# Opening weight tiles by contraction block, the last four heads projected together, rotary products on VectorE

## The chip, the cores and the metric

The kernel runs on one core of a Trainium2 chip. The metric is the device time of one execution in microseconds (us). Engines are named as in the profile: PE (TensorE, matmuls), PEld (its weight loads), DVE (VectorE), ACT (ScalarE), POOL (GpSimd) and SP (SyncE, which issues most of the DMAs).

## The reference, cut to what matters

One sequence of 512 tokens of width 1024 passes two layers. Both have a half-step SwiGLU at each end and a gated input embedding; the mixer between is a gated linear recurrence (HGRN2) in the first layer and latent attention with 16 heads in the second.

```python
for li in range(2):
    x = x + 0.5 * swiglu(rmsnorm(x, g[0]), ffn_w_in[li, 0], ffn_w_out[li, 0])
    h = rmsnorm(x, g[1])
    x = x + (hgrn2(h) if li == 0 else mla(h))
    x = x + 0.5 * swiglu(rmsnorm(x, g[2]), ffn_w_in[li, 1], ffn_w_out[li, 1])
    x = x + sigmoid(rmsnorm(x, g[3]) @ ple_w_gate[li]) * (p[li] @ ple_w_in[li])
return rmsnorm(x, final_norm)

def mla(h):                                   # k_nope, k_rope, v: made after layer 0
    c_q = rmsnorm(h @ w_dq, q_norm)           # 1024 -> 512
    q = (c_q @ w_uq).reshape(16, 128 + 64)    # per head: plain part, rotary part
    qr = concat(q1 * cos - q2 * sin, q2 * cos + q1 * sin)
    s = (q_nope @ k_nope.T + qr @ k_rope.T) * 192 ** -0.5
    return softmax(causal(s)) @ v  ->  @ w_out   # 16 heads of 128 -> 1024
```

All is float32.

## The kernel before

**Numbers.** Each float32 operand is split into a rounded part `hi` and a rest `lo`; a product is three matmuls, hi·hi, lo·hi and hi·lo (`mm3`, lines 151 to 153). `x` lies transposed, as eight tiles `x[m]` of 128 features by 512 tokens. `split` makes `hi` on ACT and `lo` on DVE (lines 166 and 167; with a gain 169 and 170).

**Weights.** The host packs all weights into 512 KB tiles of eight 128x128 blocks, in the order in which they are used (`_stream`). A tile comes by DMA into one of 5 `raw` buffers, ACT casts it to `whi`, DVE subtracts to get `wlo` (3 buffers each; lines 129 and 130, in the feed-forward parts 304 and 305). `chain` gives one 128x512 output block: for each of its input blocks an `mm3` into one of four "mm" PSUM banks. Four more banks are the "aux" ones.

**Norms.** `Stats` adds up squares of tiles (ACT squares, L183, and adds on DVE or POOL, L188). `column_sums` transposes the sum on PE (L214) and reduces it on DVE (L216); `columns` turns that into a factor (DVE L195, POOL L198); `rows` spreads it on PE (L222) and copies it out on ACT (L229). In a chain the factor is applied to the output, so that PE need not wait for it.

**Opening.** The first four output blocks of the first feed-forward part (`primed`) are made in a block of its own, whose SP and PE orders are as written (`manual_schedule`). A weight tile holds the eight input blocks of one output block, so that a tile of 512 KB is whole only for one bank. Squares are summed on PE, by 64 one-column matmuls against `ones` (`square`, L1222).

**Latent attention** (`mla`) isn't written in a fixed order: a list scheduler places its instructions by what is ready and by the order of the program. Four heads share a rotary group (`rope`): two chains, copies to SBUF (L1084, L1085), four products with cos and sin (L1086, L1090 on DVE, L1087, L1091 on POOL), a difference and a sum (L1088, L1092), splits. For head h, `scores` (h) runs ahead of `weigh` (h-1): scores in four tiles with softmax (L1142 mask and maximum on DVE, L1149 exponential on ACT, L1151 on DVE, L1152 on POOL), then transposes of the probabilities (L1163) and the product with the values. `project` multiplies a pair of heads with its part of `w_out` and adds it to `x` (L1185); for the last pair each tile is at once prepared for the next feed-forward part (`post`: split L169/L170, squares L183/L188). Between the scores of head 15 and its transposes lie the whole projection of heads 12 and 13, 48 matmuls, and part of what came before.

Of the kernel before, what the change touches and what calls it, by code (L numbers as in the profile page):

```python
# [9 lines left out]
F32 = mybir.dt.float32  # L10
F32R = mybir.dt.float32r
I32 = mybir.dt.int32
AF = mybir.ActivationFunctionType
# [3 lines left out]
P = 128  # L17
T = 512
NT = T // P
D = 1024  # L20
# [37 lines left out]
def kernel(  # L58
# [27 lines left out]
    def slot(s="s", dt=F32, tag="s"):  # L86
        return spool.tile([P, T], dt, tag=tag, bufs=BUFS[tag], name=name(s))
# [147 lines left out]
    def load(c):  # L235
        nc.sync.dma_start(x[c], xT[c * P : (c + 1) * P, :])
# [342 lines left out]
        stream["n"] = (stream["tiles"] - 2) * WB  # L579

    class Next:
        def __init__(self, cols, eng=pool):
            self.cols = cols
            self.xg = [[] for _ in cols]
            self.stats = Stats(KC, eng)

        def __call__(self, m):
            for i, col in enumerate(self.cols):
                self.xg[i].append(split(x[m], gain(col, m)))
            if self.stats.eng is not None:  # L590
                self.stats.add(x[m])

    def gcol(layer, i):
        return V_GAIN + (layer * 4 + i) * KC
# [471 lines left out]

    def mla(xg, stats, cn, krope, sin, cos, post):
        _, rb = rows(stats)
        st = Stats(4)
        cq = []  # L1070
        for m in range(4):
            ps = chain(xg)
# [3 lines left out]
            cq.append(split(c, gain(V_QN, m)))  # L1076
        rq = st.columns()
        sc = tiny()
        dve.tensor_scalar(out=sc, in0=rq, scalar1=float(192.0 ** -0.5), scalar2=None, op0=ALU.mult)

        def rope(group):
            pa, pb = chain(cq), chain(cq)
            qa, qb, ta, tb = (slot("rt") for _ in range(4))
            act.copy(qa, pa)  # L1084
            act.copy(qb, pb)  # L1085
            dve.tensor_tensor(out=ta, in0=qa, in1=cos, op=ALU.mult)  # L1086
            pool.tensor_tensor(out=tb, in0=qb, in1=sin, op=ALU.mult)  # L1087
            dve.tensor_tensor(out=ta, in0=ta, in1=tb, op=ALU.subtract)  # L1088
            h1, l1 = split(ta)
            dve.tensor_tensor(out=qb, in0=qb, in1=cos, op=ALU.mult)  # L1090
            pool.tensor_tensor(out=qa, in0=qa, in1=sin, op=ALU.mult)  # L1091
            dve.tensor_tensor(out=qb, in0=qb, in1=qa, op=ALU.add)  # L1092
            h2, l2 = split(qb)
            res = []
            for j in range(4):
                d = slot("qr", F32R)
                s = slice(32 * j, 32 * j + 32)
                for i, src in enumerate((h1, h2, l1, l2)):
                    nc.sync.dma_start(d[32 * i : 32 * i + 32, :].bitcast(F32), src[s, :].bitcast(F32))
                res.append(d)  # L1100
            return res
# [76 lines left out]

        outs = []

        def project(n, part):
            pair = outs[2 * n : 2 * n + 2]
            for m in range(part * KC // 2, (part + 1) * KC // 2):
                po = chain(pair[::-1] if n < B_HEADS // 2 - 1 else pair)
                dve.tensor_tensor(out=x[m], in0=po, in1=x[m], op=ALU.add)  # L1185
                if n == B_HEADS // 2 - 1:
                    post(m)

        qr, vals = rope(0), values(0)
        last = None  # L1190
        for h in range(B_HEADS):
            ahead = h < B_HEADS - 1
            rotated, value = qr[h % 4], vals[h % 2]
            if h % 4 == 3 and ahead:
                qr = rope(h // 4 + 1)
            if h % 2 == 1 and ahead:
                vals = values(h // 2 + 1)
            pr = scores(rotated)
            if last is not None:
                outs.append(weigh(*last))  # L1200
            last = (pr, value)
            if h > 2:
                project((h - 1) // 2 - 1, 1 - h % 2)
        project(B_HEADS // 2 - 2, 1)
        outs.append(weigh(*last))
        for part in range(2):
            project(B_HEADS // 2 - 1, part)


    first = Next([gcol(0, 0)], None)  # L1210
    primed, heads = [mm_bank() for _ in range(4)], []

    def prime(c, *ks):
        for k in ks:
            w = tuple(a[:, k * P : (k + 1) * P] for a in heads[c])
            mm3(primed[c], w, first.xg[0][k], k == 0, k == KC - 1)

    def square(m):
        sq = slot("sq", F32, "r")
        act.activation(sq, x[m], AF.Square)  # L1220
        for j in range(NT):
            pe.matmul(  # L1222
                dots[:, j : j + 1], sq[:, j * P : (j + 1) * P], ones, start=m + j == 0, stop=m == KC - 1,
                skip_group_check=True,
            )

    def head(pieces=1):
        fetch(pieces)
        heads.append(stream["ready"].pop(0))
        stream["n"] += WB  # L1230

    with tc.manual_schedule(engines={mybir.EngineType.SP, mybir.EngineType.PE}):
        dots = aux_bank()
        nc.sync.dma_start(vc, vec)
        load(0)
        first(0)
        head(4)
        prime(0, 0)
        square(0)
        for m in range(1, KC):  # L1240
            load(m)
            first(m)
            if m == 1:
                square(1)
            if m == 2:
                head(2)
                prime(0, 1, 2)
                prime(1, 0, 1, 2)
            if m == 4:
                head(2)  # L1250
                for c in range(2):
                    prime(c, 3, 4)
                prime(2, *range(5))
            if m in (2, 4):
                for k in (m - 1, m) if m == 4 else (m,):
                    square(k)
            if m == 5:
                nc.sync.dma_start(cs, cst)
            if m > 4:
                for c in range(3):  # L1260
                    if m < KC - 1:
                        prime(c, m)
                square(m)
        sums = dots[:, 0:NT]
        for c in range(3):
            prime(c, KC - 1)
        head()
# [48 lines left out]
def _rows(w):  # L1316
    k, m = w.shape
    return w.reshape(k // P, P, m // P, P).transpose(0, 2, 1, 3).reshape(-1, P, P)


def _stream(i):
    out = []

    def ffn(l, n):
        wi = i["ffn_w_in"][l, n]
        wo = i["ffn_w_out"][l, n]
        sides = [_blocks(wi[:, c : c + DFF]).reshape(NF, KC, P, P) for c in (0, DFF)]
        for lo, hi in GROUPS:
            for f in range(lo, hi):
                if f < PLAIN:  # L1330
# [55 lines left out]
    def project(n, part):  # L1386
        a, b, c = 2 * n * P, (2 * n + 1) * P, (2 * n + 2) * P
        rows = [wo[a:b], wo[b:c]]
        if n < B_HEADS // 2 - 1:
            rows = rows[::-1]  # L1390
        out.append(_blocks(np.concatenate(rows, axis=0)[:, part * D // 2 : (part + 1) * D // 2]))

    for h in range(B_HEADS):
        ahead = h < B_HEADS - 1
        if h % 4 == 3 and ahead:
            turned(h // 4 + 1)
        if h % 2 == 1 and ahead:
# [3 lines left out]
        if h > 2:  # L1401
            project((h - 1) // 2 - 1, 1 - h % 2)
    project(B_HEADS // 2 - 2, 1)
    for part in range(2):
        project(B_HEADS // 2 - 1, part)
    ffn(1, 1)
    ple(1)
    w = np.concatenate(out, axis=0)
# [64 lines left out]
```

## Time and profile before

| what | value |
|---|---|
| three runs | 2190.23, 2191.95, 2192.36 us; median 2191.95 |
| the profiled execution | 2192.49 us; its span 2190.7, so 1.8 lies around the span |
| busy share of the span | PE 99%, PEld 88%, DVE 69%, ACT 44%, POOL 15% |
| chain that ended last | PE 95%, DVE 3%, issue 1%, ACT 1% |
| DMA | 261.47 MB, 119 GB/s over the span |

The chain is followed back from the last instruction to what released each step; where a share of it belongs to PE, nothing but fewer or quicker matmuls shortens the span, and where it belongs to another engine PE stood waiting. Matmul ends are modelled, so a start-to-start distance of two equal matmuls tells more of their price than the length of one. PE's granted clock is in the views by window.

### The profile page before, as it was taken

To read this page: it belongs to the slowest core of one execution; us is meant where nothing else is said; L and a number is where in the kernel's file an instruction comes from. 1 tells how busy PE (TensorE), PEld (TensorE's weight loads), DVE (VectorE), ACT (ScalarE), POOL (GpSimd) and SP (SyncE) were. 2 spreads that over 40 slices of the span, in tenths; PEclk is the share of its full clock that TensorE was granted. 3 is DMA by queue.
4 is the path that set the end of the run, shared out by engine and by line. 5 is a ranking of instruction groups with operands and counts; after the bars stand their busy time and mean duration, and the time that the engine had idled before them with its cause. 6 is when DMAs were issued, how large, how long until landed. Compare 5 with 4: busy or idle time off the path is not lost.

```text
span 2190.7 us, 32865 instructions
## 1 busy us (share of the span) xinstructions
PE 2162.3 (99%) x13086; PEld 1935.8 (88%) x13086; DVE 1522.2 (69%) x2252; ACT 968.2 (44%) x1373; POOL 330.7 (15%) x437
## 2 busy tenths in 40 slices
PE   8999999999999999999999999999999999999998
PEld 7899998898888899998888989988888878999987
DVE  5777676777786676675766757767677776675765
ACT  5344353323235353454553525445454553443443
POOL 2000001554521000001110000022111110000011
PEclk9999999999999999999999999999999999999999
DMA  5465562212113565552234656422122134664621
GB/s 184 136 154 158 133 172 99 86 60 68 68 68 97 148 162 155 147 159 97 94 118 130 164 149 165 134 98 86 66 79 87 59 88 125 156 171 126 173 106 49
DMA packets 76106, 261.47 MB, mean 119 GB/s; under 512 B 9136, under 2 KB 11312, under 8 KB 75952
## 3 DMA queue, kind: packets, MB, share of 16 engines
q1 hardware_dynamic: 64720, 220.15, 30.5%
q0 software_dynamic: 10368, 37.75, 10.0%
q8 instruction: 103, 1.69, 0.3%
q10 hardware_dynamic: 864, 1.46, 0.2%
q14 instruction: 51, 0.42, 0.1%
HBM read 253.04 MB, written 2.10 MB: 116 GB/s over the span
## 4 chain that ended last, share of the span: by engine, by line
PE 95%; DVE 3%; issue 1%; ACT 1%; DMA 0%; POOL 0%; SPq 0%; DVEq 0%; ACTq 0%
PE aux L314 19%; PE mm L151 18%; PE mm L152 18%; PE mm L153 17%; PE mm L314 14%; PE aux L152 2%; PE aux L153 2%; PE aux L151 2%; PE aux L723 1%; PE aux L1163 1%; PE aux L1137 0%; PE aux L1138 0%; PE aux L214 0%; PE aux L1222 0%; PE aux L222 0%
## 5 line engine op out<-in xcount | busy, mean ns | idle before, releaser
L151 PE MATMUL mm<-hi,whi 128*128 128x512 f32 x1656 | 650.7, 395 | 11.4 <-ACT whi L129 7.0
L152 PE MATMUL mm<-lo,whi 128*128 128x512 f32 x1656 | 650.5, 393 | 5.2 <-DVE lo L170 3.7
L153 PE MATMUL mm<-hi,wlo 128*128 128x512 f32 x1656 | 648.3, 391 | 0.0
L305 DVE TENSOR_TENSOR wlo<-raw,whi 128x1024 fp32r<-128x1024 f32 x340 | 424.9, 1250 | 219.3 <-ACT whi L304 216.3
L304 ACT CAST whi<-raw 128x1024 fp32r<-128x1024 f32 x340 | 355.2, 1046 | 288.8 <-PE mm L152 165.5
L151 PEld LDWEIGHTS mm<-hi,whi 128*128 128x128 f32 x1656 | 312.5, 189 | 76.0 <-ACT whi L129 7.0
L152 PEld LDWEIGHTS mm<-lo,whi 128*128 128x128 f32 x1656 | 313.0, 189 | 69.4 <-DVE lo L170 5.5
L153 PEld LDWEIGHTS mm<-hi,wlo 128*128 128x128 f32 x1656 | 312.8, 189 | 63.3
L314 PE MATMUL aux<-hi,whi 128*128 128x256 f32 x1152 | 327.4, 284 | 0.1
L314 PE MATMUL aux<-hi,wlo 128*128 128x256 f32 x1152 | 325.9, 283 | 0.0
L314 PE MATMUL aux<-lo,whi 128*128 128x256 f32 x1152 | 325.9, 283 | 0.0
L314 PE MATMUL mm<-hi,whi 128*128 128x256 f32 x864 | 244.5, 283 | 0.0
L314 PE MATMUL mm<-lo,whi 128*128 128x256 f32 x864 | 244.5, 283 | 0.0
L314 PE MATMUL mm<-hi,wlo 128*128 128x256 f32 x864 | 244.5, 283 | 0.0
L314 PEld LDWEIGHTS aux<-hi,whi 128*128 128x128 f32 x1152 | 220.8, 192 | 0.8 <-ACT whi L304 0.3
L314 PEld LDWEIGHTS aux<-lo,whi 128*128 128x128 f32 x1152 | 220.9, 192 | 0.5
L314 PEld LDWEIGHTS aux<-hi,wlo 128*128 128x128 f32 x1152 | 220.9, 192 | 0.0
L288 POOL DMA_DIRECT2D raw<-in_wall x72 | 62.8, 872 | 939.6 <-DMA raw<-in_wall 645.8
L129 ACT CAST whi<-raw 128x1024 fp32r<-128x1024 f32 (+2 forms) x104 | 104.3, 1008 | 174.1 <-PE mm L152 126.5
L314 PEld LDWEIGHTS mm<-hi,whi 128*128 128x128 f32 x864 | 165.9, 192 | 0.0
L314 PEld LDWEIGHTS mm<-lo,whi 128*128 128x128 f32 x864 | 165.9, 192 | 0.0
L314 PEld LDWEIGHTS mm<-hi,wlo 128*128 128x128 f32 x864 | 165.9, 192 | 0.0
(249 smaller groups left out, 2914.3 us busy)
## 6 DMA issues: line engine op xcount, KB each, us to landing
raw<-in_wall SPq DMA_DIRECT2D x403, 512.0 KB, 3.4
raw<-in_wall POOLq DMA_DIRECT2D x72, 512.0 KB, 5.7
x<-in_xT SPq DMA_DIRECT2D x8, 256.0 KB, 6.6
qr<-hi SPq DMA_DIRECT2D x32, 64.0 KB, 2.0
qr<-lo SPq DMA_DIRECT2D x32, 64.0 KB, 2.0
out_dram<-o SPq DMA_DIRECT2D x8, 256.0 KB, 2.6
p<-in_pT ACTq DMA_DIRECT2D x4, 256.0 KB, 4.6
cs<-in_cst SPq DMA_DIRECT2D x1, 385.0 KB, 7.1
```

The costliest lines, as they stand in the source:

```text
L129: act.copy(hi[:, s], raw[:, s])
L151: pe.matmul(out, a[0], b[0], start=first, stop=False)
L152: pe.matmul(out, a[0], b[1], start=False, stop=False)
L153: pe.matmul(out, a[1], b[0], start=False, stop=last)
L288: nc.gpsimd.dma_start(self.raw, wall[self.plus], accum_op=ALU.add)
L304: act.copy(hi, self.raw)
L305: dve.tensor_tensor(out=lo, in0=self.raw, in1=hi.bitcast(F32), op=ALU.subtract)
L314: pe.matmul(o, w[u][:, s], b[i][v], start=first and e + i + n == 0, stop=False, skip_group_check=True)
L723: pe.matmul(sc[:, e * 192 : (e + 1) * 192].rearrange("p (i b n) -> p i b n", i=2, n=3 * m), k[:, j * P : (j + 1) * P], q4[:, :, j * nbt : ...
L1163: pe.transpose(banks[b][:, o : o + P], prob[i][:, j * P : (j + 1) * P], ident)
```

## The change

It has three parts, on the device and in the host's packing.

1. **Opening.** Weight tile i (of four) now holds input blocks 2i and 2i+1 of all four first output blocks. The first tile comes in two DMAs of 256 KB, between the loads of `x`. Each `x[m]` is followed by 12 matmuls, three for each of the four banks. The 64 one-column matmuls are gone; DVE adds the squares, and `column_sums` (four transposes, one reduction) gives the sum ahead of the matmuls of m = 7. A one-column activation at the start (`warm`) draws the load of ACT's table to the front.
2. **Rotary products.** L1087 and L1091 go from POOL to DVE, in four groups; so do the two adds of the latent query's squares (`Stats(4, dve)`). The small scaling L1079 goes from DVE to POOL.
3. **Last four heads.** Four banks (`half`) take heads 12 and 13, then 14, and after `weigh(15)` head 15, for the output blocks 0 to 3; blocks 4 to 7 are chains over all four heads. The matmuls are as many as before; the adds to `x` for these heads are 8, not 16.

```diff
     def mla(xg, stats, cn, krope, sin, cos, post):
-        st = Stats(4)
+        st = Stats(4, dve)
...
-        dve.tensor_scalar(out=sc, in0=rq, scalar1=float(192.0 ** -0.5), scalar2=None, op0=ALU.mult)
+        pool.tensor_scalar(out=sc, in0=rq, scalar1=float(192.0 ** -0.5), scalar2=1.0, op0=ALU.mult, op1=ALU.mult)
...
-            pool.tensor_tensor(out=tb, in0=qb, in1=sin, op=ALU.mult)
+            dve.tensor_tensor(out=tb, in0=qb, in1=sin, op=ALU.mult)
...
-            pool.tensor_tensor(out=qa, in0=qa, in1=sin, op=ALU.mult)
+            dve.tensor_tensor(out=qa, in0=qa, in1=sin, op=ALU.mult)
...
         def project(n, part):
-            pair = outs[2 * n : 2 * n + 2]
             for m in range(part * KC // 2, (part + 1) * KC // 2):
-                po = chain(pair[::-1] if n < B_HEADS // 2 - 1 else pair)
-                dve.tensor_tensor(out=x[m], in0=po, in1=x[m], op=ALU.add)
-                if n == B_HEADS // 2 - 1:
-                    post(m)
+                add(m, chain(outs[2 * n : 2 * n + 2][::-1]))
+
+        def part(ps, heads, first, last):
+            for i, h in enumerate(heads):
+                mm3(ps, block(), outs[h], first and i == 0, last and i == len(heads) - 1)
...
-            if h > 2:
+            if 2 < h < B_HEADS - 1:
                 project((h - 1) // 2 - 1, 1 - h % 2)
-        project(B_HEADS // 2 - 2, 1)
+        n = B_HEADS - 1
+        half = [mm_bank() for _ in range(KC // 2)]
+        for ps in half:
+            part(ps, (n - 3, n - 2), True, False)
+        for ps in half:
+            part(ps, (n - 1,), False, False)
         outs.append(weigh(*last))
-        for part in range(2):
-            project(B_HEADS // 2 - 1, part)
+        for m, ps in enumerate(half):
+            part(ps, (n,), False, True)
+            add(m, ps)
+            post(m)
+        for m in range(KC // 2, KC):
+            ps = mm_bank()
+            part(ps, (n - 3, n - 2, n - 1, n), True, True)
+            add(m, ps)
+            post(m)
...
-    first = Next([gcol(0, 0)], None)
+    first = Next([gcol(0, 0)], dve, False)
+    primed = [mm_bank() for _ in range(4)]
     with tc.manual_schedule(engines={mybir.EngineType.SP, mybir.EngineType.PE}):
-        dots = aux_bank()
+        warm = tiny(1)
+        act.activation(warm, ones, AF.Square)
         nc.sync.dma_start(vc, vec)
         load(0)
...
+        for i in range(4):
...
+            for e in range(2):
+                m = 2 * i + e
+                s = slice(e * WB * P // 2, (e + 1) * WB * P // 2)
+                if i == 0:
+                    nc.sync.dma_start(raw[:, s], wall[i][:, s])
+                    load(m + 1)
+                elif e == 0:
+                    nc.sync.dma_start(raw, wall[i])
+                    for k in range(m + 1, min(m + 3, KC)):
+                        load(k)
+                first(m)
...
+                first.stats.add(x[m])
+                if m == KC - 1:
+                    sums = first.stats.sums()
+                for c in range(4):
+                    w = slice(s.start + c * P, s.start + (c + 1) * P)
+                    mm3(primed[c], (hi[:, w], lo[:, w]), first.xg[0][m], m == 0, m == KC - 1)
         rb = rows(first.stats, sums)[1]
-        prime(3, *range(KC))
```

**How the order moves, on PE in the opening.** These are PE's first rows before (`mm_87` to `mm_89` are the first three banks, `whi_102` and `whi_139` the first two weight tiles, `hi_96` and `hi_122` the first two tiles of x).

```order
L151 MATMUL mm_87<-hi_96,whi_102 128x512
L152 MATMUL mm_87<-lo_97,whi_102 128x512
L153 MATMUL mm_87<-hi_96,wlo_103 128x512
L1222 MATMUL aux_93<-ones,sq_115 128x1 x4
L1222 MATMUL aux_93<-ones,sq_126 128x1 x4
L151 MATMUL mm_87<-hi_122,whi_102 128x512
...
L151 MATMUL mm_88<-hi_96,whi_139 128x512
```

And these are the first rows of it now (`mm_87` to `mm_90` are the four banks, `whi_98` the first tile).

```order
L151 MATMUL mm_87<-hi_102,whi_98 128x512
L152 MATMUL mm_87<-lo_103,whi_98 128x512
L153 MATMUL mm_87<-hi_102,wlo_99 128x512
L151 MATMUL mm_88<-hi_102,whi_98 128x512
...
L151 MATMUL mm_89<-hi_102,whi_98 128x512
...
L151 MATMUL mm_90<-hi_102,whi_98 128x512
...
L151 MATMUL mm_87<-hi_126,whi_98 128x512
```

One tile of x and one half of a weight tile now give 12 matmuls in a row, and no one-column matmul stands between.

**On DVE, at the first rotary group.** Before (`rt` are the rotary tiles, `wlo` two weight tiles' rests, `lo_14052` the rest of a key or query tile).

```order
L1086 TENSOR_TENSOR rt_13866<-rt_13864,cos_1028 128x512
L130 TENSOR_TENSOR wlo_14087<-raw_14084,whi_14086 128x1024
L1079 TENSOR_SCALAR t_13830<-t_13820 128x4
L130 TENSOR_TENSOR wlo_14229<-raw_14226,whi_14228 128x1024
L1088 TENSOR_TENSOR rt_13866<-rt_13866,rt_13867 128x512
L1090 TENSOR_TENSOR rt_13865<-rt_13865,cos_1028 128x512
L167 TENSOR_TENSOR lo_14052<-mm_14038,hi_14051 128x512
```

Now:

```order
L1086 TENSOR_TENSOR rt_13850<-rt_13848,cos_1012 128x512
L1091 TENSOR_TENSOR rt_13848<-rt_13848,sin_1011 128x512
L130 TENSOR_TENSOR wlo_14071<-raw_14068,whi_14070 128x1024
L1087 TENSOR_TENSOR rt_13851<-rt_13849,sin_1011 128x512
L130 TENSOR_TENSOR wlo_14213<-raw_14210,whi_14212 128x1024
L1088 TENSOR_TENSOR rt_13850<-rt_13850,rt_13851 128x512
L1090 TENSOR_TENSOR rt_13849<-rt_13849,cos_1012 128x512
L167 TENSOR_TENSOR lo_14036<-mm_14022,hi_14035 128x512
```

The two products with the sine stand ahead of the rest `lo` on DVE, and the scaling L1079 has left the row.

**On PE, where the projection of head 15 begins.** Before, after the head's output (`hi_17096`, `lo_17097`) come one mm3 for each of four banks and then chains of two heads.

```order
L153 MATMUL aux_17083<-ph_17075,lo_16501 128x128
L151 MATMUL mm_17100<-hi_17096,whi_17103 128x512
L151 MATMUL mm_17120<-hi_17096,whi_17103 128x512
...
L153 MATMUL mm_17150<-hi_17096,wlo_17104 128x512
L151 MATMUL mm_17165<-hi_16978,whi_17168 128x512
...
L151 MATMUL mm_17165<-hi_17096,whi_17168 128x512
```

Now (`hi_17056` is head 15; `hi_16620`, `hi_16794`, `hi_16962` are heads 12, 13, 14).

```order
L153 MATMUL aux_17043<-ph_17035,lo_16485 128x128
L151 MATMUL mm_16966<-hi_17056,whi_17002 128x512
L151 MATMUL mm_16967<-hi_17056,whi_17002 128x512
...
L153 MATMUL mm_16969<-hi_17056,wlo_17003 128x512
L151 MATMUL mm_17103<-hi_16620,whi_17106 128x512
...
L151 MATMUL mm_17103<-hi_16794,whi_17106 128x512
...
L151 MATMUL mm_17103<-hi_17056,whi_17106 128x512
```

Each of the blocks 4 to 7 is a chain of 12 matmuls now, of 6 before; the other matmuls of heads 12 and 13 for these blocks no longer stand ahead of head 15's transposes.

**On SP, the first loads.** Before, all of x (`x_79` to `x_86`) stands ahead of the fourth weight tile and what follows; now the last tile of x stands behind three more weight tiles.

```order
L1246 DMA raw_244<-in_wall 128x1024
L120 DMA raw_326<-in_wall 128x1024
L120 DMA raw_328<-in_wall 128x1024
L120 DMA raw_330<-in_wall 128x1024
L236 DMA x_86<-in_xT 128x512
```

With five `raw` buffers, `raw_328` and `raw_330` wait until the first and second tile have been converted, and `x_86` waits with them.

## Rows read from the trace of the kernel before

**Rows 1.** From the page: busy time of each engine, and the chain that ended last by engine.

```profile
PE 2162.3 (99%) x13086; PEld 1935.8 (88%) x13086; DVE 1522.2 (69%) x2252; ACT 968.2 (44%) x1373; POOL 330.7 (15%) x437
PE 95%; DVE 3%; issue 1%; ACT 1%; DMA 0%; POOL 0%; SPq 0%; DVEq 0%; ACTq 0%
```

**Rows 2.** What PE waited for, over the whole span: us in total, times, longest us.

```profile
PE mm L151 <- ACT whi L129: 7.0, 1, 7.0
PE mm L152 <- DVE lo L170: 3.7, 4, 2.8
PE mm L151 <- DVE lo L167: 2.0, 1, 2.0
PE aux L151 <- DVE t L1142: 1.5, 1, 1.5
```

**Rows 3.** The chain that ended last, in the opening: start us, us, what.

```profile
1.64 4.86 DMA raw<-in_wall
...
8.63 3.21 PE aux L1222 x16
...
18.21 0.79 PE aux L1222 x8
...
25.27 1.68 PE aux L1222 x16
...
29.15 0.79 PE aux L1222 x8
...
32.12 1.68 PE aux L1222 x16
...
35.99 0.44 PE aux L222 x4
```

**Rows 4.** PE in the opening, by the timeline: start us, us, engine, line, operation. The last row is the first after the four banks are full.

```profile
6.99 0.80 PE L151 MATMUL mm<-hi,whi 128*128 128x512 f32 x1 [6.99 <-ACT whi L129]
...
11.70 0.77 PE L151 MATMUL mm<-hi,whi 128*128 128x512 f32 x1
...
17.39 0.58 PE L152 MATMUL mm<-lo,whi 128*128 128x512 f32 x1
17.81 0.40 PE L153 MATMUL mm<-hi,wlo 128*128 128x512 f32 x1
...
41.98 0.39 PE L153 MATMUL mm<-hi,wlo 128*128 128x512 f32 x1
42.20 0.39 PE L153 MATMUL aux<-hi,wlo 128*128 128x512 f32 x1
```

**Rows 5.** ACT and DVE around the opening, by the timeline.

```profile
3.87 1.28 ACT L169 ACT_TABLE_LOAD   x1 [3.87 <-DMA x<-in_xT]
...
6.53 1.33 ACT L129 CAST whi<-raw 128x256 fp32r<-128x256 f32 x4
...
45.30 1.67 DVE L305 TENSOR_TENSOR wlo<-raw,whi 128x1024 fp32r<-128x1024 f32 x1
```

**Rows 6.** Stretches of the span: from and to, us, busy time of PE, PEld, DVE, ACT, POOL with instructions, PE's granted clock, share of the DMA engines, GB/s.

```profile
1479.00:1482.30 3.30, 3.30 (x9) 2.48 (x9) 3.06 (x5) 2.45 (x4) 0.00 (x0) 0.53 0.32 80
1776.80:1782.40 5.60, 5.53 (x15) 4.03 (x16) 4.26 (x6) 3.32 (x5) 1.48 (x2) 0.50 0.06 23
```

**Rows 7.** The first rotary group, by the timeline of DVE, POOL and PE.

```profile
1469.89 1.02 POOL L198 TENSOR_TENSOR t<-t,mhalf 128x4 f32<-128x4 f32 x1 [6.55 <-DVE t L195]
1469.99 0.69 DVE L1086 TENSOR_TENSOR rt<-rt,cos 128x512 f32<-128x512 f32 x1 [0.18 <-ACT rt L1084]
...
1470.88 1.30 POOL L1091 TENSOR_TENSOR rt<-rt,sin 128x512 f32<-128x512 f32 x1
1470.94 2.32 DVE L130 TENSOR_TENSOR wlo<-raw,whi 128x1024 fp32r<-128x1024 f32 x1 [0.26 <-ACT whi L129]
...
1473.19 1.25 DVE L1079 TENSOR_SCALAR t<-t 128x4 f32<-128x4 f32 x1
...
1477.42 0.50 PE L151 MATMUL mm<-hi,whi 128*128 128x512 f32 x1 [2.01 <-DVE lo L167]
```

**Rows 8.** Groups by line and shape in the attention layer (1440 to 1800 us): line, what, count, busy us and mean ns, idle time before.

```profile
L130 DVE TENSOR_TENSOR wlo<-raw,whi 128x1024 fp32r<-128x1024 f32 x37 | 46.3, 1251 | 14.9 <-ACT whi L129 12.7 <-PE mm L153 1.3 <-PE aux L1163 0.8
L1088 DVE TENSOR_TENSOR rt<-rt,rt 128x512 f32<-128x512 f32 x4 | 5.5, 1366 | 2.4 <-POOL rt L1087 2.4
L1090 DVE TENSOR_TENSOR rt<-rt,cos 128x512 f32<-128x512 f32 x4 | 2.7, 678 | 0.0
```

**Rows 9.** The end of the attention, by the timeline of PE and DVE: PE's waits in brackets, and the first of DVE's row of work for the next feed-forward part.

```profile
1759.12 1.21 PE L151 MATMUL mm<-hi,whi 128*128 128x512 f32 x4 [0.68 <-ACT hi L166]
...
1776.82 0.80 PE L152 MATMUL mm<-lo,whi 128*128 128x512 f32 x1 [2.77 <-DVE lo L170]
...
1760.83 2.48 DVE L1185 TENSOR_TENSOR x<-mm,x 128x512 f32<-128x512 f32 x4 [1.04 <-PE mm L153]
1763.23 0.74 DVE L170 SCALAR_TENSOR_TENSOR lo<-x,vc,hi 128x512 fp32r<-128x512 f32 x1
```

**Rows 10.** The softmax of head 15, from the last matmul of its scores to its transposes: two pieces of the chain and the last step on POOL by the timeline.

```profile
1739.39 0.23 PE aux L1138
...
1745.51 0.69 POOL L1152 TENSOR_SCALAR P<-P,t 128x512 f32<-128x512 f32 x1 [2.11 <-DVE t L1151]
...
1752.84 0.98 PE aux L1163 x9
```

More of the change, by code (lines that the diff above doesn't have):

```diff
@@ L581, with __init__ @@
     class Next:
-        def __init__(self, cols, eng=pool):
-            self.cols = cols
+        def __init__(self, cols, eng=pool, sums=True):
+            self.cols, self.sums = cols, sums
             self.xg = [[] for _ in cols]
@@ L589, in __call__ @@
                 self.xg[i].append(split(x[m], gain(col, m)))
-            if self.stats.eng is not None:
+            if self.sums:
                 self.stats.add(x[m])
@@ L1179, in mla, with add @@
         outs = []
+        def add(m, po):
+            dve.tensor_tensor(out=x[m], in0=po, in1=x[m], op=ALU.add)
         def project(n, part):
-            pair = outs[2 * n : 2 * n + 2]
             for m in range(part * KC // 2, (part + 1) * KC // 2):
-                po = chain(pair[::-1] if n < B_HEADS // 2 - 1 else pair)
-                dve.tensor_tensor(out=x[m], in0=po, in1=x[m], op=ALU.add)
-                if n == B_HEADS // 2 - 1:
-                    post(m)
+                add(m, chain(outs[2 * n : 2 * n + 2][::-1]))
+        def part(ps, heads, first, last):
+            for i, h in enumerate(heads):
+                mm3(ps, block(), outs[h], first and i == 0, last and i == len(heads) - 1)
         qr, vals = rope(0), values(0)
@@ L1201, in mla @@
             last = (pr, value)
-            if h > 2:
+            if 2 < h < B_HEADS - 1:
                 project((h - 1) // 2 - 1, 1 - h % 2)
-        project(B_HEADS // 2 - 2, 1)
-        outs.append(weigh(*last))
-        for part in range(2):
-            project(B_HEADS // 2 - 1, part)
-    first = Next([gcol(0, 0)], None)
[L1211 to L1230, printed above, removed]
+        n = B_HEADS - 1
+        half = [mm_bank() for _ in range(KC // 2)]
@@ L1232 @@
+    primed = [mm_bank() for _ in range(4)]
     with tc.manual_schedule(engines={mybir.EngineType.SP, mybir.EngineType.PE}):
-        dots = aux_bank()
+        warm = tiny(1)
+        act.activation(warm, ones, AF.Square)
         nc.sync.dma_start(vc, vec)
         load(0)
[L1236 to L1267, printed above, removed]
+        for i in range(4):
+            stream["tiles"] += 1
+            stream["n"] += WB
+            raw = wpool.tile([P, WB * P], F32, tag="raw", bufs=5, name=name("raw"))
+            hi = wpool.tile([P, WB * P], F32R, tag="whi", bufs=3, name=name("whi"))
+            lo = wpool.tile([P, WB * P], F32R, tag="wlo", bufs=3, name=name("wlo"))
+            for e in range(2):
[9 more added lines that the diff above has]
+                first(m)
+                for n in range(2) if m == 0 else (None,):
+                    c = s if n is None else slice(s.start + n * 2 * P, s.start + (n + 1) * 2 * P)
+                    act.copy(hi[:, c], raw[:, c])
+                    dve.tensor_tensor(out=lo[:, c], in0=raw[:, c], in1=hi[:, c].bitcast(F32), op=ALU.subtract)
+                if m == 5:
+                    nc.sync.dma_start(cs, cst)
+                first.stats.add(x[m])
[4 more added lines that the diff above has]
+                    mm3(primed[c], (hi[:, w], lo[:, w]), first.xg[0][m], m == 0, m == KC - 1)
@@ L1329, in ffn @@
             for f in range(lo, hi):
-                if f < PLAIN:
+                if l + n == 0 and f < 2:
+                    if f == 0:
+                        out.append(np.stack([side[g] for g in range(2) for side in sides], axis=1).reshape(-1, P, P))
+                elif f < PLAIN:
                     out.extend(side[f] for side in sides)
@@ L1400, in _stream @@
         out.append(_blocks(wq[:, h, :128]))
-        if h > 2:
+        if 2 < h < B_HEADS - 1:
             project((h - 1) // 2 - 1, 1 - h % 2)
-    project(B_HEADS // 2 - 2, 1)
-    for part in range(2):
-        project(B_HEADS // 2 - 1, part)
+    tail = wo[-4 * P :]
+    out.append(_rows(tail[: 2 * P, : D // 2]).reshape(2, KC // 2, P, P).transpose(1, 0, 2, 3).reshape(-1, P, P))
+    out.append(_rows(tail[2 * P : 3 * P, : D // 2]))
+    out.append(_rows(tail[3 * P :, : D // 2]))
+    out.append(_blocks(tail[:, D // 2 :]))
     ffn(1, 1)
```

## The prediction

> **What bounds the kernel now.** I read the page's busy shares and the chain by engine first [rows 1]: PE works 2162.3 of 2190.7 us and 95% of the chain is PE's. So only three things can shorten the span: fewer PE instructions, shorter waits of PE, or matmuls that run at the higher of PE's two clock levels for longer. The reader is to see that the 28.4 us in which PE is idle are all there is to win by hiding. The list of PE's waits comes next [rows 2]: 7.0 us before the first weight tile, 3.7 for the rest of x (L170), 2.0 for a rest `lo` (L167). The change touches all three places, so I took each one's stretch of the timeline: the opening [rows 3 to 5], the first rotary group [rows 7, 8], the end of the attention [rows 9, 10]. [...]
>
> **The opening.** Before, the four banks are full when the first other matmul after them starts, at 42.20 [rows 4]; two matmuls of the next block already stand ahead of that, which leaves 42.20 - 0.46 = 41.74. The parts of the change:
>
> - Squares. The five groups of L1222 in the chain take 3.21 + 0.79 + 1.68 + 0.79 + 1.68 = 8.15 us [rows 3]. In their place come four transposes, as the four of L222: 0.44 [rows 3]. ACT squares x as before; DVE's seven adds, at about 0.68 each like a two-operand row of this shape [rows 8], lie beside PE's 2.7 to 5.1 us per tile of x. Gain 7.7.
> - Start. The first weight DMA lands at 6.50, 4.86 after its issue, and with 512 KB [rows 3]. A half lands between 3.9 (when x, 256 KB, issued before it, is there [rows 5]) and 6.50; I take 5.2, the middle. ACT's table load, 1.28 us at 3.87 [rows 5], is done before by `warm`, so ACT isn't what is late. The first cast piece takes from 6.53 to PE's start at 6.99 [rows 4, 5]; so PE starts at about 5.6: gain 1.4, bounds 0 and 2.6.
> - Clock. Before, dense matmuls ran from 11.70 to 17.8 at the low level, 6.1 us, then it rose [rows 4]; 18 matmuls were paid at it. The new opening is dense from 5.6 on, so by 6.1 us it rises at 11.7, after 14.3 matmuls: 3.7 x 0.2 = 0.7. If it rises at 17.8 whatever PE does, 28.6 are paid: a loss of 2.1. If it rises after 3.5 us as in the attention [rows 6], 8.2 are paid: a gain of 2.0.
>
> Checked as a whole: 14.3 x 0.427 + 81.7 x 0.2275 = 24.7, with 5.6 and the transposes of L214 and L222, 0.9, gives 31.2 against 41.7, 0.7 more than the three parts; that is the first matmul behind each pause or group, which takes longer than its like (0.80 at 6.99, 0.77 at 11.70 [rows 4]). **Gain 10.5**, bounds 7 (late clock, half the earlier start) and 12.
>
> What could be late then: 12 matmuls (2.7 us) now lie between the sum's transposes and L222, for a reduction, a scaling and the power on POOL (1.02 [rows 7]): just enough. Behind L222, 48 matmuls = 10.9 us cover the work of ACT and DVE up to the third weight tile of the next block. Before, that tile's rest ended at 45.30 + 1.67 = 46.97 [rows 5], 11.0 after L222 began at 35.99. It would be needed 11.8 after: 0.8 us of slack, so I cost it at nothing and at up to 1.5 where DVE's new order delays it. The last tile of x waits on SP behind three weight tiles; I reckon its landing at about 20 and its use after 26.
>
> **The rotary products.** PE waits 2.01 us until 1477.42 for a rest `lo` on DVE, and 9 matmuls at the low level follow [rows 6, 7]. In DVE's row before it one weight rest took 2.32 and the 128x4 scaling L1079 1.25, while L1091 and L1087 ran on POOL; the mean of the rest's kind is 1.25 [rows 7, 8]. In the new order DVE does L1086, L1091, rest, L1087, rest, L1088, L1090, `lo`, from 1469.99 on: six at about 0.6 from start to start and two at 1.15 is 5.9, so `lo` ends at about 1475.9 instead of 1477.37 and PE restarts at 1476.0. That gains 1.4, and leaves a wait of 0.6. Behind a wait of 0.68 four matmuls took 1.21, no slow ones; behind 2.01 and 2.77 they were slow [rows 6, 7, 9]; so I take the slow 9 x 0.2 = 1.8 as gone too. **Gain 3**, bounds 0 (the wait stays, in another place) and 3.2. In the other three groups DVE gets 1.2 us more work and L1088 no longer waits or stretches (mean 1366 ns, its sister L1090 678 [rows 8]); PE waits at none of them before, so that is nothing, bounds -2 and 0.
>
> [...] But L1086 began 0.1 after L198 and took 0.69, no more than alone [rows 7, 8]: a 128x4 instruction on POOL doesn't hold DVE up here. The measurement decides, and I keep 3.
>
> **The last four heads.** Before, PE waits 0.68 and then 3.7 in four pieces, the last of 2.77, for DVE, which works without a break from 1760.83 on: eight adds and eight times a split and a sum of squares, while PE sends a finished tile every six matmuls, 1.36 us [rows 2, 9]. One such tile costs DVE about 0.62 + 0.65 + 0.6 = 1.87. Then 13 slow matmuls cost 13 x 0.2 = 2.6 [rows 6]. In all 7.2 with the small gap ahead of them. After, blocks 4 to 7 come 2.73 us apart, longer than the 1.87; four tiles at once, 7.5 us of DVE, lie beside 48 matmuls, 10.9. So the 3.7 and 2.6 go. What is late next: the transposes of head 15. The softmax took from 1739.39 to 1746.20, 6.6 after the last score matmul, and had until 1752.84 [rows 10]. With 36 matmuls in between instead of 60, 8.2 us and the product for head 14, it is ready at about the moment that PE wants it; I reckon a wait of 0.8 at the probabilities' rests and 0.75 at head 15's split (it is there before, 0.68). **Gain 5**, bounds 1 (a wait of 2 with a slow stretch) and 7.
>
> In the middle of the attention the scheduler shuffles rows; I take -1, bounds -3 and 0.
>
> **Sum.** 10.5 + 3 + 5 - 1 = 17.5 off the profiled execution's 2192.5 gives 2175.0. That execution lies 0.5 above the median of the runs, so the forecast is 2174.5, own range 2169 to 2181.
>
> **Rivals.**
>
> 1. Only part of the opening: the clock rises late, the first half-tile comes as late as the whole one did, and the third tile of the next block is waited for. The opening gains 10.5 - 2.8 - 1.4 - 1 = 5.3, the rest is as above: 2180. For it speaks that the low level lasted until 17.8 once; against it that after every wait of the attention it rose within 6 us of work.
> 2. The attention gives nothing: the wait moves from the one rest to another, as DVE has 5 us more of rotary products and PE the same matmuls. Only 10.5 - 1 is left: 2182.5. DVE's 69% speak for it, against it that it stood beside POOL and not before it.
> 3. Slower: the softmax of the last heads and the rotary groups become what PE waits for. Each of the five places (four groups, the tail) costs a wait of 2 and a slow stretch of 1.8 to 2.6, as at 1477.42, together 20; with the opening's 10.5 that makes 2201. It decides itself where a wait grows from the 0.68 that left the clock alone towards the 2.01 that didn't; DVE's addition is 1.2 per group and L1088's stretch falls away.
> 4. No change: 1 and 2 together, gain 5.3 - 1 - 1: 2188.6.
>
> [...]
>
> **How the numbers follow.** Forecast 0.57, rival 1 0.15, rival 2 0.16, rival 3 0.05, rival 4 0.07. What a measurement can tell from no change is 0.2%, 4.4 us. Faster (below 2187.6): 0.57 + 0.15 + 0.16 = 0.88; same: rival 4, 0.07; slower: rival 3, 0.05. The range 2167 to 2185 holds the forecast, rivals 1 and 2, less some of their edges; 2167 needs the upper bounds of the clock, the start and the tail together.
>
> **What would show it.** The opening: first matmul at 5.6, no L1222, twelve matmuls per tile of x, distances halved at about 11.7, L222 at about 30.5 with no wait ahead of it. The rotary group: POOL without L1087 and L1091, rests of 1.2 beside it, PE's wait there near 0.6 and no slow stretch behind it. The end: no wait for L170, two waits under 0.9 ahead of head 15's matmuls, the clock at 1.00 throughout. Wrong would be a longer wait with slow matmuls at any of these places, or slow matmuls until 17.8 in the opening.

## The result, and the profile after

The changed kernel takes 2176.14 us (median; 2175.48 to 2176.89, 4 runs) against 2191.09 (2189.11 to 2192.36, 4 runs): ratio 0.9933, 95% interval 0.9921 to 0.9945, that is 15.0 us less. The forecast was 2174.5, the range 2167 to 2185. The profiled execution took 2175.48, its span is 2173.7, 17.0 less than that of before. But the profiled execution of before (2192.49) was slower than all four of its runs, and that of the changed kernel was the fastest of its four, so some 2 of the 17.0 are the spread between runs. The total came out as forecast; the parts didn't.

The page's busy shares and its chain by engine, the two rows that answer to [rows 1]:

```profile
PE 2148.8 (99%) x13026; PEld 1925.5 (89%) x13026; DVE 1522.3 (70%) x2261; ACT 968.5 (45%) x1374; POOL 313.3 (14%) x428
PE 94%; DVE 3%; ACT 1%; issue 1%; DMA 0%; POOL 0%; SPq 0%; POOLq 0%; DVEq 0%; ACTq 0%
```

PE works 13.5 us less, and is idle for 24.9 instead of 28.4. What it waits for, in the changed kernel (us, times, longest), answers to [rows 2]:

```profile
PE mm L151 <- ACT whi L1252: 5.6, 1, 5.6
PE aux L314 <- ACT mm L465: 2.5, 1, 2.5
...
PE aux L151 <- DVE t L1142: 1.5, 1, 1.5
...
PE mm L151 <- DVE lo L167: 0.7, 1, 0.7
PE aux L152 <- DVE pl L1168: 0.7, 3, 0.2
PE mm L151 <- ACT hi L166: 0.7, 1, 0.7
```

The start is 1.4 earlier, the waits for L170 are gone, that for L167 is 0.7 of 2.0. The second row is new: 2.5 us for ACT's L465, which no row before had.

Where the 17.0 come from is read by setting the same DVE instruction of both traces side by side. The first product with the factor rb (L389) comes 7.8 us earlier than before; the first latent query tile (L1074), at 1447.6 instead of 1454.4, 6.8 earlier; the first L389 behind the attention, at 1771.0 instead of 1788.0, 17.0 earlier. So 6.8 came ahead of the attention and 10.2 in it; I had 10.5 and 7. Finer steps are read from PE's order: where both traces have had the same rows, in number and kind, the starts of the next row are compared ("by matched rows").

**The opening.** PE by the timeline, answering to [rows 4]:

```profile
5.56 0.79 PE L151 MATMUL mm<-hi,whi 128*128 128x512 f32 x1 [5.56 <-ACT whi L1252]
...
9.14 0.63 PE L153 MATMUL mm<-hi,wlo 128*128 128x512 f32 x1
9.57 0.47 PE L151 MATMUL mm<-hi,whi 128*128 128x512 f32 x1
9.87 0.40 PE L152 MATMUL mm<-lo,whi 128*128 128x512 f32 x1
...
26.69 0.60 PE L214 MATMUL aux<-cs,sq 128*128 128x128 f32 x4
...
29.88 0.60 PE L222 MATMUL aux<-cs,t 128*128 128x128 f32 x4
...
60.57 0.39 PE L314 MATMUL aux<-hi,whi 128*128 128x256 f32 x1 [2.53 <-ACT mm L465]
```

The distances halve at about 9.7 (0.43 to 0.23), after some 9.6 slow matmuls, and the next block begins at 30.24, behind the spread. Against 41.74 that is 11.5 earlier, more than the 10.5 forecast. Then PE waits 2.53 at 60.57, and a stretch follows in which a dozen 256-column matmuls start 0.21 apart instead of 0.12 (PE's granted clock is 0.61 from 60 to 64.3).

By matched rows PE is 11.4 ahead of before up to the last matmul ahead of this wait (57.76 against 69.14), and 6.8 ahead when the slow stretch is over (64.29 against 71.06). It stays at 6.8 up to the attention. So this one place costs 4.6: 2.7 at the wait, 0.8 about a second one of 0.24 for the weight rest L300, 1.1 of slow matmuls. Windows of the changed kernel (from and to, busy of each engine, PE's granted clock, DMA share, GB/s):

```profile
50.00:100.00 50.00, 46.65 (x276) 41.41 (x275) 37.50 (x49) 18.79 (x24) 1.74 (x2) 0.97 0.46 132
1440.00:1500.00 60.00, 59.28 (x322) 51.32 (x321) 43.46 (x88) 32.73 (x57) 6.78 (x11) 1.00 0.33 102
1500.00:1530.00 30.00, 28.19 (x156) 24.10 (x155) 21.13 (x57) 15.87 (x35) 4.26 (x8) 1.00 0.26 79
1740.00:1790.00 50.00, 49.33 (x226) 40.86 (x225) 35.91 (x54) 30.42 (x45) 8.36 (x9) 1.00 0.34 97
```

The attention's three windows are all at 1.00 now; before, they were at 0.97, 0.94 and 0.93:

```profile
1440.00:1500.00 60.00, 57.99 (x291) 48.84 (x290) 37.59 (x68) 28.52 (x47) 11.32 (x12) 0.97 0.30 97
1500.00:1530.00 30.00, 28.43 (x160) 24.93 (x160) 22.87 (x62) 17.91 (x40) 9.91 (x11) 0.94 0.25 71
1740.00:1790.00 50.00, 45.52 (x204) 35.80 (x203) 36.63 (x62) 25.97 (x44) 8.55 (x9) 0.93 0.21 63
```

**The wait at 60.57.** The chain of the changed kernel ahead of it, without PE (start us, us, what):

```profile
55.17 1.20 DVE lo L167 x2
56.38 0.61 DVE g L389
...
57.07 0.64 ACT g L390
...
57.73 0.70 DVE g L394
...
58.98 1.06 ACT whi L299
...
60.07 1.24 DVE wlo L300
```

DVE and ACT hand each tile to one another. L465, which copies out the bank that PE adds to next, stands on ACT behind L299. This ping-pong starts when the norm's factor rb is copied out, at 30.52, 29.4 ahead of L465; before, it took 29.7 (37.25 to 66.93). But before, the copy ended 1.75 ahead of the matmul that needs it:

```profile
66.93 0.58 ACT L465 COPY mm<-aux 128x512 f32<-128x512 f32 x1
69.26 0.28 PE L314 MATMUL aux<-hi,whi 128*128 128x256 f32 x1
```

The change brings PE to this place 11.4 earlier and the copy only 7.0: 11.4 - 7.0 - 1.75 leaves 2.65 to wait.

### The profile page after: what moved, and what is told of

The parts are those of the page before. It is cut to its first block, busy times and chain, and to the rows that moved or that the text cites. A ratio compares the mean times of both kernels' runs of the same rounds, so it can differ in the third digit from the quotient of the medians.

```text
span 2173.7 us, 32746 instructions
## 1 busy us (share of the span) xinstructions
PE 2148.8 (99%) x13026; PEld 1925.5 (89%) x13026; DVE 1522.3 (70%) x2261; ACT 968.5 (45%) x1374; POOL 313.3 (14%) x428
## 3 DMA queue, kind: packets, MB, share of 16 engines
q8 instruction: 102, 1.67, 0.3%
## 4 chain that ended last, share of the span: by engine, by line
PE 94%; DVE 3%; ACT 1%; issue 1%; DMA 0%; POOL 0%; SPq 0%; POOLq 0%; DVEq 0%; ACTq 0%
PE aux L314 19%; PE mm L151 18%; PE mm L152 18%; PE mm L153 17%; PE mm L314 14%; PE aux L152 1%; PE aux L153 1%; PE aux L723 1%; PE aux L151 1%; PE aux L1163 1%; PE aux L1138 0%; PE aux L1137 0%; ACT whi L304 0%; PE aux L214 0%; DVE wlo L305 0%
## 5 line engine op out<-in xcount | busy, mean ns | idle before, releaser
L304 ACT CAST whi<-raw 128x1024 fp32r<-128x1024 f32 x340 | 355.2, 1046 | 288.3 <-PE mm L152 163.5
L129 ACT CAST whi<-raw 128x1024 fp32r<-128x1024 f32 x95 | 99.8, 1051 | 171.7 <-PE mm L152 113.1
```

The lines of the kernel that those rows point to most:

```text
L129: act.copy(hi[:, s], raw[:, s])
L304: act.copy(hi, self.raw)
```

## Experiments

Each is timed in 5 rounds beside the kernel before (medians 2189.7 to 2190.7). The changed kernel (2176.14) wasn't timed again beside them; since the kernel before moved by up to 1.4 from 2191.09, a difference of about 1 us from 2176.14 rests on the traces and not on the times. "By the trace" means the same DVE instruction in two traces. Diffs are against the changed kernel where nothing else is said.

### opening_only and attention_only

The new opening with the old attention, and the reverse.

```diff
 # opening_only: the opening and its packing as in the change, mla() as before
 # attention_only: mla() and its packing as in the change, the opening as before
```

> The new opening on the old attention. If the two traces' shift is to be believed (the same work on DVE is 11.5 us earlier when the four banks are full, 7.0 us earlier after the wait of 2.53 us at 60.57, and stays at 7 up to the attention), the gain is 7.0 and the time 2184.1, with a PE wait of about 2.5 us for ACT L465 at 60.6 and slow matmuls behind it. The rival (the opening's 10.5 of the prediction is there in full, and the attention gave less than the traces show): 2180.6.

> The old opening on the new attention. By the shift between the traces the attention brings 10.0 (4.0 at the first rotary group and the wait after it, 6.0 at the last heads): 2181.1, no wait for L170, and no wait of PE for ACT L465 at about 70. The rival (the attention gives the 7 of the prediction, the rest is the opening's): 2184.1. If the two parts don't add up, this and opening_only together miss 2176.1.

Measured: opening_only 2187.34 (ratio 0.9989, 0.998 to 0.9997), attention_only 2182.93 (0.9967, 0.9954 to 0.9979). Together they bring 3.2 + 7.6 = 10.8, the change some 14 to 15: they don't add up. opening_only missed both of its forecasts, and attention_only lies between its two. The trace of opening_only tells why. At 61 it has the new wait, 2.5, and up to the attention it is 5.7 ahead; in the attention, whose code is that of before, it loses 2.6 of them. It has waits there that before doesn't have (of the first row, 2.0 was there before, and 0.5 is at the last rotary group):

```profile
PE mm L151 <- DVE lo L167: 2.5, 2, 2.0
...
PE aux L152 <- DVE pl L1168: 0.9, 3, 0.5
...
PE aux L214 <- DVE sq L188: 0.7, 1, 0.7
...
PE aux L153 <- DVE lo L167: 0.5, 1, 0.5
PE aux L151 <- ACT hi L166: 0.5, 1, 0.5
```

Compared row by row, PE's order in its attention isn't that of before, although no line of that code differs: the list scheduler's choices there depend on what the opening left it. attention_only has an order of its own too; it differs from the changed kernel's in some 500 rows of PE, and its attention is 9.1 ahead of before's by the trace, not 10.2. Its opening, the very code of before, is 1.3 ahead of before's: there 11 matmuls at the start are slow (the next starts more than 0.33 later), in before's trace 17.

### early_sums and x8_first

early_sums: the sum's transposes ahead of m = 6, the spread ahead of m = 7. x8_first: the last tile of x ahead of the fourth weight tile on SP.

```diff
 # early_sums, PE's order at the end of the opening
+L214 sums ; 12 matmuls of m = 6 ; L222 spread ; 12 matmuls of m = 7
-12 matmuls of m = 6 ; L214 sums ; 12 matmuls of m = 7 ; L222 spread
 # x8_first
-                    for k in range(m + 1, min(m + 3, KC)):
+                    for k in ((3, 4), (5, 6, 7), ())[i - 1]:
```

> The changed kernel with the sum's four transposes one tile of x earlier and the spread L222 ahead of the last 12 matmuls of the opening instead of behind them. Theory: the wait of 2.53 at 60.57 is the end of a chain on ACT and DVE that starts when the norm's factor rb is copied out (30.52) and whose links wait for each other; it starts 2.9 us earlier then, the wait and the slow matmuls behind it (some 4 us together) go: 2172.2, between 2171.5 and 2173.5. Rival 1: the wait is for weights (DMA or a raw buffer): same time, 2176.1. Rival 2: the chain is bound by PE's own tiles, not by rb: same time.

> The changed kernel with the last tile of x loaded ahead of the fourth weight tile and of the three tiles it stood behind on SP. Theory: the last tile of x lands at about 20.7 and isn't used by PE before 26.7, so it bounds nothing: 2176.1 within 0.7. Rival: the late tile of x delays DVE's and ACT's rows (they idle 1.2 us for it) and with them the chain to 60.57: 2174 to 2175.

Measured: early_sums 2173.86 (2173.55 to 2174.46), 0.4 above the range expected; x8_first 2176.51 (2175.9 to 2176.65). In early_sums ACT copies rb out at 28.31, 2.2 earlier, and PE's waits at this place are

```profile
59.02 0.39 PE L314 MATMUL aux<-hi,whi 128*128 128x256 f32 x1 [0.48 <-ACT mm L465]
59.80 0.39 PE L314 MATMUL aux<-hi,wlo 128*128 128x256 f32 x1 [0.28 <-DVE wlo L300]
```

with the granted clock at 1.00 there (50 to 100). L465 ends 1.55 earlier (58.97 instead of 60.52), and PE comes to this place 0.5 later, since it now waits 0.37 for POOL ahead of the spread; so the wait shrank by 2.05. Nothing about the weights was changed: the chain from rb is the bound, and both rivals fall. By the trace early_sums reaches the attention 2.8 ahead of the changed kernel; it has attention_only's order of the attention, row for row, and loses 1.1 of it there. The tile of x that SP delays bounds nothing: x8_first still waits 2.5 for L465.

### rope_pool and scale_dve

```diff
 # rope_pool
-            dve.tensor_tensor(out=tb, in0=qb, in1=sin, op=ALU.mult)
+            pool.tensor_tensor(out=tb, in0=qb, in1=sin, op=ALU.mult)
-            dve.tensor_tensor(out=qa, in0=qa, in1=sin, op=ALU.mult)
+            pool.tensor_tensor(out=qa, in0=qa, in1=sin, op=ALU.mult)
 # scale_dve
-        pool.tensor_scalar(out=sc, in0=rq, scalar1=float(192.0 ** -0.5), scalar2=1.0, op0=ALU.mult, op1=ALU.mult)
+        dve.tensor_scalar(out=sc, in0=rq, scalar1=float(192.0 ** -0.5), scalar2=None, op0=ALU.mult)
```

> The changed kernel with the two rotary products L1087 and L1091 back on POOL; the scaling stays on POOL. Theory: what made PE wait 2.01 before is POOL's products, in two ways: DVE's weight rest beside them takes 2.3 instead of 1.2, and L1088 stands behind them; PE's wait goes from 0.72 to about 2 and slow matmuls can follow: 2178 to 2180. Rival: the order of DVE's row and the scaling on it did it; then the wait stays below 1 and the time is 2176.1 within 0.7.

> The changed kernel with the scaling L1079 (128x4) back on DVE, the rotary products stay on DVE. Theory: the 1.25 us that L1079 took before came from the POOL product beside it; without one it takes under 0.2 on DVE, the wait stays below 1: 2176.1 within 0.7. Rival: it costs DVE over 1 us wherever it stands: wait 1.8 and 2177.2, with slow matmuls 2179.

Measured: rope_pool 2179.47 (2178.36 to 2180.46), 3.3 more than the changed kernel. Its first rotary group, DVE, POOL and PE by the timeline:

```profile
1464.77 3.45 DVE L130 TENSOR_TENSOR wlo<-raw,whi 128x1024 fp32r<-128x1024 f32 x2 [0.26 <-ACT whi L129]
1469.40 0.69 DVE L1088 TENSOR_TENSOR rt<-rt,rt 128x512 f32<-128x512 f32 x1 [1.18 <-POOL rt L1087]
...
1464.70 1.30 POOL L1091 TENSOR_TENSOR rt<-rt,sin 128x512 f32<-128x512 f32 x1
1466.08 1.06 POOL L1079 TENSOR_SCALAR t<-t 128x4 f32<-128x4 f32 x1
1467.22 2.15 POOL L1087 TENSOR_TENSOR rt<-rt,sin 128x512 f32<-128x512 f32 x1
...
1471.35 0.50 PE L151 MATMUL mm<-hi,whi 128*128 128x512 f32 x1 [2.10 <-DVE lo L167]
```

Both ways of the theory are there: the two weight rests take 3.45 together, and L1088 waits 1.18 for POOL (in the kernel before it had no such wait; there L1079 stood on DVE and not between POOL's two products). In the changed kernel the same stretch reads

```profile
1464.59 1.22 DVE L130 TENSOR_TENSOR wlo<-raw,whi 128x1024 fp32r<-128x1024 f32 x1
...
1466.33 1.22 DVE L130 TENSOR_TENSOR wlo<-raw,whi 128x1024 fp32r<-128x1024 f32 x1
...
1464.25 0.49 POOL L1079 TENSOR_SCALAR t<-t 128x4 f32<-128x4 f32 x1
...
1469.40 0.50 PE L151 MATMUL mm<-hi,whi 128*128 128x512 f32 x1 [0.72 <-DVE lo L167]
```

By matched rows this group is 1.8 of rope_pool's 3.3. Some 1.2 more are lost at the last rotary group, where DVE's L1086 and L1088 run beside POOL's products in 1.78 and 1.67 instead of 0.68, and PE waits again:

```profile
1653.07 1.78 DVE L1086 TENSOR_TENSOR rt<-rt,cos 128x512 f32<-128x512 f32 x1
...
1655.11 1.67 DVE L1088 TENSOR_TENSOR rt<-rt,rt 128x512 f32<-128x512 f32 x1
...
1662.20 0.47 PE L151 MATMUL mm<-hi,whi 128*128 128x512 f32 x1 [0.49 <-DVE lo L167]
```

opening_only has the same wait there (0.48), the kernel before, whose order is another one, has none. So not all of the 3.3 is what the change gained on the rotary products.

scale_dve took 2177.39 (2176.17 to 2177.45). Here its L1079 takes 0.16 on DVE, so the 1.25 of before [rows 7] came from POOL's product beside it (there L1087, 2.27 from 1472.14 on), as the theory said; the wait is 0.80. That the time is 1.2 longer all the same, near the rival's figure, isn't the scaling: by the trace 1.15 is lost in the attention behind it, where the scheduler took attention_only's order on PE, row for row, and 0.9 ahead of it, where more matmuls are slow behind the wait for L465 (the granted clock is 0.93 from 50 to 100, in the changed kernel 0.97). Moving the scaling was worth nothing at its own place.

### pair_tail

The last four heads in pairs, as before.

```diff
 # project(), the tail of mla() and its packing as before; all else as in the change
```

> The changed kernel with the last four heads projected in pairs as before. Theory: PE sends a finished tile every 1.36 us, DVE needs 1.87 for it; the waits for L170 (3.7, the longest 2.77) and slow matmuls behind them come back: 5.5 to 6 more, 2182. Rival: the old tail was late for another reason (the rotary products' load on POOL, the order of rows), and with the rest of the change it costs 2 or less: 2178.

Measured: 2184.87 (2184.14 to 2186.84), 8.7 more, where 5.5 to 6 were expected. The waits are those of [rows 2, 9] again, 3.7 in four pieces with a last one of 2.77:

```profile
1762.02 0.39 PE L151 MATMUL mm<-hi,whi 128*128 128x512 f32 x1
1762.72 0.50 PE L152 MATMUL mm<-lo,whi 128*128 128x512 f32 x1 [0.31 <-DVE lo L170]
1763.05 0.39 PE L153 MATMUL mm<-hi,wlo 128*128 128x512 f32 x1
...
1770.05 0.50 PE L152 MATMUL mm<-lo,whi 128*128 128x512 f32 x1 [2.77 <-DVE lo L170]
1772.61 1.08 PE L214 MATMUL aux<-cs,sq 128*128 128x128 f32 x4 [0.20 <-DVE sq L188]
```

The mechanism stands: PE feeds tiles faster than DVE prepares them (one every 1.36 against some 1.87). The size is off by about 3, and matched rows tell where it lies; the attention of this trace is 9.8 behind the changed kernel's.

- 1.7 are lost far ahead of the edit, by slow matmuls behind the wait for L1142 (1500 to 1530 is at 0.94), where PE's order is still that of the changed kernel.
- 0.9 is lost about the softmax of the last heads, with a wait of 0.53 for L167 that the changed kernel doesn't have.
- 7.2 are lost from the first wait for L170 on, where 5.5 to 6 were expected. The pause that the profile counts as 0.31 makes the start-to-start distance 0.70 (1762.02 to 1762.72) and the next one 0.33, each 0.23 without it: 0.57 in all. So priced, the four pauses cost some 5.1 instead of 3.7, and the slow matmuls 2.1 (the granted clock is 0.97 from 1740 to 1790, in the changed kernel 1.00).

### no_warm and squares_pe

```diff
 # no_warm
-        warm = tiny(1)
-        act.activation(warm, ones, AF.Square)
 # squares_pe
-                first.stats.add(x[m])
-                if m == KC - 1:
-                    sums = first.stats.sums()
+                sq = slot("sq", F32, "r")
+                act.activation(sq, x[m], AF.Square)
+                for j in range(NT):
+                    pe.matmul(dots[:, j : j + 1], sq[:, j * P : (j + 1) * P], ones, ...)
```

> The changed kernel without the one-column activation at the start. Theory: ACT loads its table when the first tile of x has landed (3.9), the first split and with it the first cast end some 1.3 later, PE starts at about 6.9 and all of the opening, the chain to 60.57 with it, is 1.3 later: 2177.4. Rival: PE's start waits for the half weight tile at 5.1 and the table load fits beside it: 2176.1 to 2176.6.

> The changed kernel with the squares summed on PE again (64 one-column matmuls, eight ahead of each pair of tiles of x, as before), in the new layout. Theory: they are on PE's path and nothing hides them, since the chain to 60.57 begins behind them too: the four banks are full 7.7 later (8.15 less the 0.44 of the transposes), and the time is 2183.9, plus up to 1.1 if the scheduler's order of the attention is the dearer one. Rival: the wait of 2.5 at 60.57 takes up part of them: 2179 to 2181.

Measured: no_warm 2177.64 (2177.43 to 2178.48), 1.5 more; PE starts at 6.83 instead of 5.56, and the 1.3 are never made good. squares_pe 2183.11 (2182.92 to 2183.65), 7.0 more. By the trace it is 8.7 behind at the attention, 8.4 by matched rows just ahead of L465, and the wait for L465 is as long as ever (the first row; the others are the first of PE's timeline):

```profile
PE aux L314 <- ACT mm L465: 2.5, 1, 2.5
...
5.29 1.87 PE L1260 MATMUL aux<-ones,sq 128*128 128x1 f32 x8 [5.29 <-ACT sq L1258]
7.02 0.77 PE L151 MATMUL mm<-hi,whi 128*128 128x512 f32 x1
```

So nothing hides the squares, as the theory has it; the first group even stands ahead of PE's start, which is 7.02 instead of 5.56. Of the 0.7 above 7.7, 2.4 more slow matmuls at the start are 0.5. The rest may come from its eight groups, one ahead of each tile's matmuls, where before had five; that wasn't tried. (Its expectation says "each pair of tiles"; the kernel has one group of eight matmuls per tile.)

### early_v56

early_sums one tile of x further, with x8_first's load.

```diff
+L214 sums ; matmuls of m = 5 ; L222 spread ; matmuls of m = 6 and 7
-matmuls of m = 5 and 6 ; L214 sums ; matmuls of m = 7 ; L222 spread
```

> early_sums taken one tile of x further: the last tile of x is loaded ahead of the fourth weight tile, the sum's transposes stand ahead of the matmuls of m = 5, the spread ahead of those of m = 6. The scheduler then gives the attention the very order of the changed kernel, and not that of early_sums and attention_only. Theory: the wait of 0.5 and 0.3 that early_sums kept at 58 goes, and the attention is 1.1 shorter by its order alone: 2172.0, between 2171.3 and 2172.8. Rival: the 1.1 came from the chip's run, not from the order: 2173.1 to 2173.9.

Measured: 2172.65 (2172.26 to 2173.2), ratio 0.9919 (0.9906 to 0.9933): the fastest, 3.5 below the changed kernel. The wait for L465 is gone, 0.27 for L300 is left, and at the attention it is 3.75 ahead of the changed kernel. But in the attention it lost 1.7 of that in the profiled execution, with the same order of rows: the windows show a slow stretch behind the wait for L1142 that the changed kernel has without one.

```profile
1500.00:1530.00 30.00, 28.21 (x140) 24.13 (x140) 19.93 (x52) 15.79 (x33) 3.81 (x8) 0.94 0.21 66
```

So of theory and rival neither is shown whole, though the time lies in the theory's range: the order of attention_only, early_sums and scale_dve costs 1.1 against the other order without that slow stretch, and is 0.6 quicker than it with one. And L465 comes only 2.6 earlier here (57.37), though rb is copied out 5.3 earlier (25.18): taken this far, rb is no longer all that bounds the chain, and what else does wasn't tried.

## Why the prediction was right, and where it was wrong

That the total was right is luck: the opening gave 3.7 less than forecast and the attention 3.2 more. The parts, by matched rows of the two profiled executions:

- **Opening: 10.5 forecast, 6.8 kept.** It brought 11.4, and 4.6 of them were lost at 60. Start (5.56), halves and table load (1.28 from 3.95 on in no_warm) came as worked out, and so, nearly, did the squares (7.7 forecast; squares_pe 8.4). The distances halved after 9.6 slow matmuls, not 14.3, which gave 1 more. The 0.427 and 0.2275 of the sum are near what before's trace shows: ten distances from 12.70 to 16.97 make 4.27, fifteen from 38.80 to 42.20 make 3.40. But neither trace shows the low clock that the forecast and rival 1 have in the opening: the granted clock reads 1.00 there (before from 11.70 to 17.81, now from 5.56 to 9.57), and only the distances tell slow matmuls from quick ones. The step that failed is the sentence on what could be late: I followed ACT and DVE only to the third weight tile behind L222, which indeed was no wait, and costed the rest at nothing (the slack of 0.8 that I gave even that tile counts both groups of transposes; with L222 alone behind the sum it is 0.4). The chain from rb runs on to L299 and L465, 29 us behind L222 (29.88 to 58.98; before 35.83 to 65.97, 30 us). Before, the 24 matmuls of the fourth bank, 5.5 us, stood behind L222 and covered its end; in the new layout all four banks are full ahead of it. That cost 2.7 + 0.8 + 1.1, where I had allowed up to 1.5. The wait is 2.5 to 2.6 in each of the eight traces that have the new opening with the spread behind m = 7; what it costs in all isn't fixed: the traces with the very opening of the changed kernel keep 5.7 (opening_only) to 7.1 (pair_tail), as more or fewer matmuls are slow. And the 18 slow matmuls that I read before are one trace's: attention_only has fewer with the same opening and is 1.3 quicker there.
- **Rotary products: 3 forecast, 3.0 found.** The wait went from 2.01 to 0.72 (1.3), and the slow stretch behind it, 1.8, went too. rope_pool brought back the wait but not the slow stretch, so of the 3.0 it shows 1.8. The scaling on POOL took 0.49; L1091 and the rest beside it took 0.69 and 1.22 on DVE, as much as in scale_dve, which has no scaling on POOL.
- **Last heads: 5 forecast, 7.5 found.** The waits for L170 and the slow matmuls went, 0.68 at head 15's split stayed, and the 0.8 that I had added for the softmax didn't come. The term that was mis-sized is the waits: I took the profile's idle time, 3.7, where by the distances of the starts around them they cost some 5 (pair_tail). The terms that I added to 7.2 there, 0.68 + 3.7 + 2.6, make 7.0, which less 0.8 and 0.75 leaves 5.4.
- **Middle: -1 forecast, -0.4 found.** 1.5 were lost by the scheduler's order, in which three waits of 0.22 to 0.24 came in. But the wait of 1.53 for L1142, which I left as it is, was followed by slow matmuls before (1.1) and not after; early_v56, with the changed kernel's order there, has them, so this gain is one of chance.

Rival 1's figure (5.3 for the opening) was nearer, by another mechanism: not a late clock but the cover of the chain.

## What to carry to other kernels

When work that stands ahead of a dependency is moved in front of it, follow the dependent chain on the other engines to its end, not to the first tile that needs it: what was moved may have been the cover of something 30 us later. Where a list scheduler orders a part, two edits don't add up, even if they lie 1400 us apart: compare the order of the untouched part before a difference of one or two microseconds is put down to the edit. Where one engine feeds another, give it chains longer than the other's work per tile (2.73 instead of 1.36 against 1.87 here). And price a pause by the distances of the starts around it, not by the idle time alone.

## What was not expected of the hardware

The same wait isn't always followed by a low granted clock. Behind the 1.53 for L1142 at the same place, matmuls were slow before, in pair_tail and in early_v56 (0.62 from 1515.5 to 1520 before; 0.94 from 1500 to 1530 in all three), and not in the changed kernel, x8_first and no_warm (1.00). Behind 2.01 the stretch was slow before and in opening_only (0.97 from 1440 to 1500 in both), behind the 2.10 of rope_pool not (1.00):

```profile
1440.00:1500.00 60.00, 57.74 (x316) 49.76 (x315) 41.66 (x81) 32.77 (x58) 14.74 (x15) 1.00 0.32 98
```

At the start of the new opening the number of slow matmuls (distances above 0.33) was between 7 and 12; it differs even between traces of kernels with the very same opening, 7 in scale_dve and 12 in opening_only. So a slow stretch of 1 to 2 us behind a wait can be a matter of chance in a single profile: in the sum its gain or loss is better written as a range than as a term.
